# Dilated attention in a hybrid decoder layer: distant keys by residue modulo four

## The chip, the cores and the metric

The kernel runs on one core of a Trainium2 chip. The metric is the device time of one execution in microseconds; a program's time is the median of several runs. Five engines work side by side and wait for each other by semaphores: TensorE (PE in the profile, with PEld for the loading of weights), VectorE (DVE), ScalarE (ACT), GpSimd (POOL) and SyncE (SP), whose queue issues most DMA transfers.

## What is computed

One decoder layer over a sequence of 1024 positions with 1024 channels. A projection of the normalised input feeds three groups of heads: four HGRN2 heads, four heads of dilated attention and four RWKV-7 heads. Their outputs go through an output projection, then a gated MLP with a short convolution, a gate with a per-layer embedding, and a final norm. The part that matters here:

```python
SW_PATTERNS = ((128, 1), (512, 4), (2048, 16))

def dilated_window_mix(q_raw, k_raw, v_raw):
    ...
    for window, dil in SW_PATTERNS:
        o, lse = banded_causal_attention(stride_gather(q, dil), stride_gather(k, dil),
                                         stride_gather(v, dil), window // dil)
        outs.append(stride_scatter(o, B_, dil))
        lses.append(stride_scatter(lse, B_, dil))
    wts = jax.nn.softmax(jnp.stack(lses, 0), axis=0)
    o = jnp.sum(wts[..., None] * jnp.stack(outs, 0), axis=0)
```

A query at position l meets, in the first pattern, all keys from l-128 to l; in the second, every fourth key back to l-512; in the third, every sixteenth back to l-2048, which is beyond the start of the sequence. The mixture by softmax denominators equals one softmax over all keys, in which a key counts as often as there are patterns that hold it (0 to 3). So further back than 128 positions a query meets only keys whose distance is a multiple of four.

## The kernel before

All work in this kernel is laid out by channel: tiles are 128 channels (two attention heads of 64) by positions. The input projection's products (`dp`, `zp`) are split into three products of a reduced fp32 type; the attention works on plain fp32.

**Where attention stands.** `phase_mix` (line 310) first runs RWKV, then interleaves four generators by hand (line 331): A and B are two chains of HGRN2 heads, C is the attention (`swa`, line 1238), F the last four columns of the input projection (`project_late`, line 526), which fill TensorE in the first half. `TURNS` (line 347) says in which of 38 rounds C gets a turn, `LATE` (line 348) in which F does. This interleaving is the program order; a scheduler then orders each engine's instructions from it and may move ready ones ahead. Behind the interleaving stands the output projection, whose first row (`first_rows`, line 336, tile `dp`) takes the heads in the order of `OUT` (line 334).

**Attention.** The heads come in two pairs, p = 0 and 1. For each pair eight query blocks of 128 positions (`qb` 0 to 7) are run through three steps, one turn apart:

- `swa_scores` (line 1285): query block `qb` against all keys from 0 to the end of its own block, for two heads (`HEADS`: partitions 0 to 63 and 64 to 127), into two PSUM tiles `swq` of the large kind (`dps`, two buffers in all). On DVE one instruction (line 1303) adds a mask, `swmask`, and finds the row's minimum; on ACT one (line 1305) takes the exponential and its sum, giving `lg`. The mask is -1e30 for keys that no pattern holds, and 8 log(count) for the others. All of `swmask` is a window into one array of 1024 columns, moved by 128 per block.
- `swa_turn` (line 1310): `lg` is transposed by TensorE in pieces of 128x128 (tile `swt`, the small PSUM kind `mx`, four buffers) and copied to `pT`, the first 512 keys by ACT and the rest by DVE.
- `swa_values` (line 1323): values (`sV`, turned once per pair in `swa_values_in`, line 1273) times `pT`, one matmul per key block and head, into `swo`, then copied by DVE to the output tile `ob`. After every fourth block `swa_out` (line 1338) divides by the sums, which `widen` and `spread2` (lines 185 and 190, tile `swd`) bring to every channel.

Per head pair this makes 36 pairs of 128x128 blocks, of which a large part holds mostly keys that are masked out.

**Queries and keys.** Queries, keys and values come from the input projection: `project_done` (line 485) scales a projected column by the norm's factor into `zst`, stores it to memory, and `swa_load` (line 1269) brings it back. Columns 24 and 27 are the queries of the two pairs.

Of the kernel before, what the change touches and what calls it, by code (L numbers as in the profile page):

```python
# [10 lines left out]
F32 = mybir.dt.float32  # L11
# [3 lines left out]
ALU = mybir.AluOpType  # L15
# [27 lines left out]
def shape_constants():  # L43
# [14 lines left out]
    c[:, CC_RU:CC_RU + P] = same & (ff % 64 >= 32) & (pp % 64 < 32)  # L58
    u = np.arange(T)[None, :]
    d = pp - (u - 896)  # L60
    cnt = ((d >= 0) & (d <= 128)).astype(np.float64)
# [18 lines left out]
class Trunk:  # L80
# [229 lines left out]
    def phase_mix(self):  # L310
# [8 lines left out]
        with self.pool("hg") as slots, self.pool("sw") as sp:  # L319
            self.slots, self.NSLOT = slots, 11  # L320
            with tc.issue_after(self.squared):
                self.hgrn_setup()
            self.sp = sp
            self.swmask = sp.tile([P, T], F32, name="swmask")
# [155 lines left out]
    def pending(self, what):  # L480
        go = self.pend.pop(what, None)
        if go:
            go()

    def project_done(self, j, ps, staged=False):
        t = self.keep.tile([P, T], F32, tag="zst", name=self.nm("zst"), bufs=2)
        kind = (j - 8) % 4 if j < 24 else 2
        parts = [(t, ps, self.R)]
        if j < 24 and kind < 3:
# [36 lines left out]
    def project_late(self, js):  # L526
# [3 lines left out]
        for i, j in enumerate(js):  # L530
# [6 lines left out]
            for hf in (0, 1):  # L537
# [3 lines left out]
                r = self.R[:, hf * HT:(hf + 1) * HT]  # L541
                self.finish(kind, t[:, dst], *((ps[:, ::-1], r[:, ::-1]) if turn and hf else (ps, r)))
                nc.sync.dma_start(d[:, dst], t[:, dst])
# [694 lines left out]
    def swa(self, sp):  # L1238
# [6 lines left out]
        for p in (0, 1):  # L1245
            d = ds[p]
            for qb in range(10):
# [5 lines left out]
                if qb == p:  # L1253
                    self.swa_values_in(d)
                if qb > 1:
                    fin = self.swa_values(sp, d, *pend.pop(0))
                if 0 < qb < 9:
                    pend[-1:] = [self.swa_turn(sp, *pend[-1])]
                if qb < 8:
# [13 lines left out]
    def swa_values_in(self, d):  # L1273
        nc, vc = self.nc, d["v"]
        V = self.sp.tile([P, T], F32, tag="sd", name=self.nm("sV"), bufs=1)
        for hf in (0, 1):
# [3 lines left out]
            nc.scalar.copy(V[:, hf * HT:(hf + 1) * HT], pt)  # L1280
        d["V"] = V.rearrange("p (b c) -> p b c", c=P)

    HEADS = slice(0, 64), slice(64, 128)

    def swa_scores(self, sp, d, qb):
        nc = self.nc
        qi, nk = qb % 4, (qb + 1) * P
        if qi == 0:
            d["den"] = sp.tile([P, 16], F32, tag="sden", name=self.nm("sden"), bufs=2)
        den = d["den"]  # L1290

        pq = [self.dps.tile([P, T], F32, tag="dp", name=self.nm("swq")) for _ in self.HEADS]
        for b in range(0, nk, HT):
            w = min(HT, nk - b)
            for h, hs in enumerate(self.HEADS):
                nc.tensor.matmul(pq[h][:, b:b + w], d["q"][hs, qb * P:nk], d["k"][hs, b:b + w], start=True, stop=True)  # L1296
        lgs = []
        for h in (0, 1):
            lg = sp.tile([P, T], F32, tag="lg", name=self.nm("lg"), bufs=4)
            nm = den[:, 8 + 2 * qi + h:9 + 2 * qi + h]  # L1300

            m0 = 896 - qb * P
            nc.vector.tensor_tensor_reduce(lg[:, :nk], pq[h][:, :nk], self.swmask[:, m0:m0 + nk],
                                           -0.125, 3e38, ALU.add, ALU.min, nm)
# [4 lines left out]

    def swa_turn(self, sp, qb, den, lgs):  # L1310
        nc, nk, pT = self.nc, (qb + 1) * P, []
        for lg in lgs:
            t = sp.tile([P, T], F32, tag="pT", name=self.nm("pT"), bufs=2)
            pT.append(t)
            for b in range(0, nk, HT):
                w = min(HT, nk - b)
                pt = self.mxp.tile([P, HT], F32, tag="mx", name=self.nm("swt"))
                for kb in range(w // P):
                    nc.tensor.transpose(pt[:, kb * P:(kb + 1) * P], lg[:, b + kb * P:b + (kb + 1) * P], self.ident)  # L1319
                (nc.vector.tensor_copy if b else nc.scalar.copy)(t[:, b:b + w], pt[:, :w])  # L1320
        return qb, den, pT

    def swa_values(self, sp, d, qb, den, pT):
        nc = self.nc
        if qb == 0:
            d["o"] = self.keep.tile([P, T], F32, tag="zst", name=self.nm("ob"), bufs=2)
        o = d["o"]
        po = self.mxp.tile([P, P], F32, tag="mx", name=self.nm("swo"))

        for kb in range(qb + 1):  # L1330
            for h, hs in enumerate(self.HEADS):
                nc.tensor.matmul(po[hs, :], d["V"][:, kb, hs], pT[h][:, kb * P:(kb + 1) * P], start=kb == 0, stop=kb == qb)  # L1332
        nc.vector.tensor_copy(o[:, qb * P:(qb + 1) * P], po)
        if qb % 4 == 3:
# [3 lines left out]
    def swa_out(self, d, qb, o, den):  # L1338
# [3 lines left out]
        os = slice((qb - 3) * P, (qb + 1) * P)  # L1342
        nc.vector.tensor_tensor(o[:, os], o[:, os], pd, ALU.mult)
        if qb == 7:
# [704 lines left out]
```

## Time and profile before

| | us |
|---|---|
| median of 3 runs | 1426.47 |
| lowest and highest run | 1426.33, 1426.6 |
| the profiled execution | 1426.57 |
| its span (first to last instruction) | 1424.8 |

The mean granted clock of TensorE in the profiled execution is 0.997. The profile comes from that one execution. A line names the source line, the engine, the operation, the tile written and the tiles read, the shape and the count; the busy time of a group is the union of its instructions. "idle before" is what the engine waited for just ahead of them. Two records of a matmul stand for one matmul of plain fp32 operands, one record for a transpose or a matmul of the reduced type. `64*128` ahead of a shape is the part of the array in use: rows (contracted partitions) by columns (output partitions).

### The profile page before, as it was taken

Reading aid. Unit: us, or ns where it says so; the run is one execution under the profiler, and the core shown is the slowest. Engines: PE = TensorE matmul, PEld = TensorE weight load, DVE = VectorE, ACT = ScalarE, POOL = GpSimd, SP = SyncE. Lnnn points to the kernel's source line nnn. Section 1 sums busy time; section 2 is a strip of 40 time slices with the busy share of each in tenths; the row PEclk is TensorE's granted clock in tenths of the full one; section 3 lists DMA queues with packets and bytes.
Section 4 is the critical chain, followed back from the end, with each engine's and each line's share of the span. In section 5 each row is a group of like instructions: output and inputs, shape, how many; then the busy total and the mean of one; then the engine's idle time right before and its main releaser. Section 6 shows DMA issues by size and latency. Waiting matters only on the chain.

```text
span 1424.8 us, 20276 instructions
## 1 busy us (share of the span) xinstructions
PE 1410.4 (99%) x7406; PEld 1166.4 (82%) x7406; DVE 1089.2 (76%) x1679; ACT 648.5 (46%) x1207; POOL 446.1 (31%) x360
## 2 busy tenths in 40 slices
PE   9999999999999999999999999999999999999997
PEld 7888887888877877888888888888888888888886
DVE  7667576674786787448998889888988799777685
ACT  7531443214535676335544444343444445455552
POOL 2221442124421331222245445454543000002343
PEclk9999999999999999999999999999999999999998
DMA  5233021230350320374332333333233973352343
GB/s 212 78 97 104 31 75 59 85 115 30 105 185 31 119 82 31 123 262 156 140 113 83 100 105 102 112 111 103 97 108 115 347 257 102 105 164 59 121 151 135
DMA packets 80019, 167.84 MB, mean 118 GB/s; under 512 B 20080, under 2 KB 22256, under 8 KB 79920
## 3 DMA queue, kind: packets, MB, share of 16 engines
q1 hardware_dynamic: 66144, 145.97, 31.0%
q10 hardware_dynamic: 12832, 17.04, 3.6%
q0 software_dynamic: 944, 3.54, 0.7%
q8 instruction: 58, 0.95, 0.3%
q14 instruction: 41, 0.34, 0.1%
HBM read 120.12 MB, written 46.40 MB: 117 GB/s over the span
## 4 chain that ended last, share of the span: by engine, by line
PE 93%; DVE 3%; ACT 2%; DMA 1%; issue 1%; POOL 0%; SPq 0%; DVEq 0%; ACTq 0%; POOLq 0%
PE bg L1465 17%; PE bv L1465 13%; PE dp L130 9%; PE dp L132 8%; PE dp L134 8%; PE bg L1787 7%; PE bv L1787 7%; PE hsc L1124 2%; PE swq L1296 2%; PE bv L130 1%; PE bv L132 1%; PE bv L134 1%; PE swt L1319 1%; PE swo L1332 1%; PE bg L132 1%; PE bg L130 1%
## 5 line engine op out<-in xcount | busy, mean ns | idle before, releaser
L130 PE MATMUL dp<-xh,whi 128*128 128x512 f32 x544 | 196.8, 407 | 0.0
L132 PE MATMUL dp<-xl,whi 128*128 128x512 f32 x544 | 188.0, 391 | 1.0 <-DVE xl L393 1.0
L134 PE MATMUL dp<-xh,wlo 128*128 128x512 f32 x544 | 188.3, 391 | 0.0
L108 POOL TENSOR_TENSOR wlo<-wraw,whi 128x512 fp32r<-128x512 f32 x63 | 89.3, 1421 | 245.2 <-ACT whi L106 237.4
L108 POOL TENSOR_TENSOR wlo<-raw,whi 128x512 fp32r<-128x512 f32 x84 | 135.7, 1634 | 73.9 <-ACT whi L106 73.9
L1465 PE MATMUL bg<-t,whi 128*128 128x512 f32 x352 | 132.4, 389 | 0.0
L106 ACT CAST whi<-wraw 128x512 fp32r<-128x512 f32 x120 | 72.6, 617 | 119.2 <-PE dp L132 73.8
L134 PEld LDWEIGHTS dp<-xh,wlo 128*128 128x128 f32 x544 | 102.1, 188 | 22.1 <-issue 0.5
L132 PEld LDWEIGHTS dp<-xl,whi 128*128 128x128 f32 x544 | 102.1, 188 | 20.8 <-DVE xl L393 1.6
L130 PEld LDWEIGHTS dp<-xh,whi 128*128 128x128 f32 x544 | 101.5, 188 | 21.5 <-issue 3.0
L108 POOL TENSOR_TENSOR wlo<-s,whi 128x512 fp32r<-128x512 f32 x44 | 66.0, 1500 | 161.6 <-ACT whi L106 150.7
L106 ACT CAST whi<-s 128x512 fp32r<-128x512 f32 x66 | 39.0, 621 | 123.2 <-PE bg L1465 115.2
L1787 PE MATMUL bg<-t,whi 128*128 128x512 f32 x308 | 94.9, 389 | 0.0
L1787 PE MATMUL bv<-t,whi 128*128 128x512 f32 x308 | 94.9, 389 | 0.0
L106 ACT CAST whi<-raw 128x512 fp32r<-128x512 f32 x88 | 52.6, 619 | 91.6 <-issue 48.5
L175 POOL TENSOR_TENSOR rst<-rst,mhalf 128x4 f32<-128x4 f32 (+1 forms) x9 | 10.3, 1145 | 219.7 <-DVE rst L173 219.7
L1465 PEld LDWEIGHTS bg<-t,whi 128*128 128x128 f32 x352 | 66.1, 188 | 13.7
L1783 ACT CAST t<-t 128x512 fp32r<-128x512 f32 x77 | 47.8, 622 | 47.7 <-PE bv L1787 29.4
L108 DVE TENSOR_TENSOR wlo<-wraw,whi 128x512 fp32r<-128x512 f32 x57 | 43.6, 768 | 31.5 <-ACT whi L106 27.6
L1787 PEld LDWEIGHTS bv<-t,whi 128*128 128x128 f32 x308 | 57.8, 188 | 12.0
L1787 PEld LDWEIGHTS bg<-t,whi 128*128 128x128 f32 x308 | 57.8, 188 | 11.9
L1465 PE MATMUL bg<-t,wlo 128*128 128x512 f32 x176 | 67.2, 389 | 0.0
(448 smaller groups left out, 3609.2 us busy)
## 6 DMA issues: line engine op xcount, KB each, us to landing
raw<-in_ffn_up_dram SPq DMA_DIRECT2D x44, 512.0 KB, 3.6
wraw<-in_w_in_dram SPq DMA_DIRECT2D x29, 512.0 KB, 3.6
z<-zst SPq DMA_DIRECT2D x18, 512.0 KB, 2.7
gb<-ct SPq DMA_DIRECT2D x33, 256.0 KB, 2.3
t<-gb SPq DMA_DIRECT2D x33, 256.0 KB, 2.8
t<-gt SPq DMA_DIRECT2D x33, 256.0 KB, 2.7
zl<-z SPq DMA_DIRECT2D x16, 512.0 KB, 4.7
wraw<-in_ple_gate_dram SPq DMA_DIRECT2D x16, 512.0 KB, 3.5
```

Source lines behind the costliest of these rows:

```text
L106: nc.scalar.copy(hi, src)
L108: eng.tensor_tensor(lo, src, hi.bitcast(F32), ALU.subtract)
L130: nc.tensor.matmul(ps[hf], wh, xh[hf], start=first, stop=False)
L132: nc.tensor.matmul(ps[hf], wh, xl[hf], start=False, stop=False)
L134: nc.tensor.matmul(ps[hf], wl, xh[hf], start=False, stop=last)
L1124: nc.tensor.matmul(sc[:, c, :], ks[:, c * P:(c + 1) * P], view(qt, c * P, [2 * n, 64 // n], [HT + n, 2], [1, n]), start=True, stop=True)
L1296: nc.tensor.matmul(pq[h][:, b:b + w], d["q"][hs, qb * P:nk], d["k"][hs, b:b + w], start=True, stop=True)
L1319: nc.tensor.transpose(pt[:, kb * P:(kb + 1) * P], lg[:, b + kb * P:b + (kb + 1) * P], self.ident)
L1332: nc.tensor.matmul(po[hs, :], d["V"][:, kb, hs], pT[h][:, kb * P:(kb + 1) * P], start=kb == 0, stop=kb == qb)
L1465: nc.tensor.matmul(ps, w[part == 2][:, s], X[k][part == 1], start=start and k == part == 0, stop=k == 3 and part == 2, skip_group_check=no ...
L1783: nc.scalar.copy(xh, x)
L1787: nc.tensor.matmul(ps[m], wt[part == 2][:, m * P:(m + 1) * P], (xh, xl)[part == 1], start=k == part == 0, stop=k == NK - 1 and part == 2)
```

## The change

Only the attention changes, with the layout of its queries.

**Far keys.** For a query block `qb` of 2 or more, keys two or more blocks back are met by residue modulo four: the 32 queries of a block whose position has residue r meet only the keys of residue r, a quarter of them. `qb // 2 * 64` keys per residue are taken, so 64, 64, 128, 128, 192, 192 for `qb` 2 to 7. Per block that is four residues by two heads, eight matmuls of 64 rows by 32 columns; keys are read with a step of four. For even `qb` this takes in the block before the query's own, which the mask then leaves out.

**Near keys.** The block's own keys and the block before are met densely, 256 keys (128 for `qb` 0). Far and near logits stand side by side in one PSUM tile, 128 to 448 columns per head, the two heads in one tile of the large kind. One masked minimum and one exponential run over both.

**Queries in classes.** Within each block of 128, queries are stored by residue (`classes`), so that a residue's 32 queries are neighbours. The scaling of columns 24 and 27 writes them so, and the result's copy and division (`plain`) put the positions back.

**Turning and values.** Transposes fall from 144 to 92. `swa_values_in` also turns the values by residue, into `F` (16 transposes and four copies over both pairs). Values are taken for two blocks at a time: the key block that both meet goes as one matmul of 256 columns, the two others as 128 each, the far ones as 64 columns (32 queries of two blocks) per residue and head. The first head's turned weights are copied by ACT, the second's by DVE.

The core of the diff (line numbers in the rows below it are those of the changed kernel):

```diff
     def swa_scores(self, sp, d, qb):
         nc = self.nc
-        qi, nk = qb % 4, (qb + 1) * P
+        qi, w = qb % 4, 64 * (qb // 2)
+        near = slice(max(qb - 1, 0) * P, (qb + 1) * P)
+        nk = w + near.stop - near.start
...
-        pq = [self.dps.tile([P, T], F32, tag="dp", name=self.nm("swq")) for _ in self.HEADS]
-        for b in range(0, nk, HT):
-            w = min(HT, nk - b)
+        pq = self.dps.tile([P, 2, HT], F32, tag="dp", name=self.nm("swq"))
+        self.uid += 1
+        for r in range(4 if w else 0):
             for h, hs in enumerate(self.HEADS):
-                nc.tensor.matmul(pq[h][:, b:b + w], d["q"][hs, qb * P:nk], d["k"][hs, b:b + w], start=True, stop=True)
+                q0 = qb * P + 32 * r
+                nc.tensor.matmul(pq[32 * r:32 * r + 32, h, :w], d["q"][hs, q0:q0 + 32], d["k"][hs, r:4 * w:4],
+                                 start=True, stop=True)
+        for h, hs in enumerate(self.HEADS):
+            nc.tensor.matmul(pq[:, h, w:nk], d["q"][hs, qb * P:(qb + 1) * P], d["k"][hs, near], start=True, stop=True)
...
+        cols = [w + b * P for b in range(2 if qb else 1)] + [b * P for b in range((w + 64) // P)]
+        for lg, t, copy in zip(lgs, d["pT"], (nc.scalar.copy, nc.vector.tensor_copy)):
+            pt = self.mxp.tile([P, HT], F32, tag="mx", name=self.nm("swt"))
+            for i, c in enumerate(cols):
+                nc.tensor.transpose(pt[:, i * P:(i + 1) * P], lg[:, c:c + P], self.ident)
+            copy(t[:, qb % 2, :len(cols) * P], pt[:, :len(cols) * P])
...
+            nc.tensor.matmul(po[hs], d["V"][:, q0, hs], both, start=True, stop=False)
+        for e, kb in ((0, q0 - 1), (1, q0 + 1))[not q0:]:
             for h, hs in enumerate(self.HEADS):
-                nc.tensor.matmul(po[hs, :], d["V"][:, kb, hs], pT[h][:, kb * P:(kb + 1) * P], start=kb == 0, stop=kb == qb)
-        nc.vector.tensor_copy(o[:, qb * P:(qb + 1) * P], po)
+                nc.tensor.matmul(po[hs, e, :], d["V"][:, kb, hs], pT[h][:, e, e * P:(e + 1) * P], start=False,
+                                 stop=not w and e == 1)
+        for f in range((w + 64) // P):
+            n = min(P, w - f * P)
+            for r in range(4):
+                c = (2 + f) * P + 32 * r
+                for h, hs in enumerate(self.HEADS):
+                    nc.tensor.matmul(po[hs, :, 32 * r:32 * r + 32], d["F"][:n, f, r, hs], pT[h][:n, :, c:c + 32],
+                                     start=False, stop=(f + 1) * P >= w and r == 3)
+        os = slice(q0 * P, (q0 + 2) * P)
+        nc.vector.tensor_copy(self.plain(o[:, os]), self.classes(po.rearrange("p e q -> p (e q)")))
```

The scheduler also orders the rows anew. The first place is on PE, in the second head pair, at the scores of query block 6. Before, two tiles (`swq_5065` and `swq_5066`) hold the two heads; `hsc` are scores of an HGRN2 head, `swd` the spreading of the sums:

```order
L1296 MATMUL swq_5065<-zl_4085,zl_4348 128x512
L1124 MATMUL hsc_5037<-qt_4609,ks_4972 128x128 x4
L1124 MATMUL hsc_5048<-qt_4963,ks_4991 128x128 x4
L1296 MATMUL swq_5066<-zl_4085,zl_4348 128x512
L193 MATMUL swd_5059<-cst,par 128x128 x4
L1296 MATMUL swq_5065<-zl_4085,zl_4348 128x384
L1296 MATMUL swq_5066<-zl_4085,zl_4348 128x384
```

In the changed kernel, the same engine around block 6 (`swq_5049`) and the end of block 5 (`swq_4974`); `32x128` and `32x192` are far matmuls of one residue and head, `128x256` near ones:

```order
L1324 MATMUL swq_4974<-zl_4100,zl_4341 32x128
L1351 MATMUL swt_4924<-cst,lg_4848 128x128 x3
L1324 MATMUL swq_4974<-zl_4100,zl_4341 32x128
L1138 MATMUL hsc_4929<-qt_4577,ks_4877 128x128 x4
L1324 MATMUL swq_4974<-zl_4100,zl_4341 32x128 x6
L1327 MATMUL swq_4974<-zl_4100,zl_4341 128x256 x2
L1324 MATMUL swq_5049<-zl_4100,zl_4341 32x192 x8
L1327 MATMUL swq_5049<-zl_4100,zl_4341 128x256 x2
```

Block 6 stands together now, eight far matmuls and two near ones, where the heads' first 512 keys were parted before; block 5's eight far matmuls are in three pieces with other work between them. In the whole new order, six of the twelve far sets are cut, into nine pieces more than sets, and four of the sixteen near pairs are parted.

The second place is on PE too, where the first row of the output projection (`dp`) begins, in the second head pair. Before, around the turning of block 6 (`swt_5205` to `swt_5223`) and the outputs of an HGRN2 head (`hpo`):

```order
L1319 MATMUL swt_5205<-cst,lg_5071 128x128 x4
L1319 MATMUL swt_5211<-cst,lg_5071 128x128 x3
L130 MATMUL dp_5503<-xh_4701,whi_5499 128x512
L130 MATMUL dp_5503<-xh_4685,whi_5499 128x512
L1319 MATMUL swt_5217<-cst,lg_5074 128x128 x4
L1319 MATMUL swt_5223<-cst,lg_5074 128x128 x3
```

In the changed kernel, around the turning of the same block (`swt_5178` and `swt_5184`):

```order
L137 MATMUL dp_5441<-xl_4670,whi_5437 128x512
L137 MATMUL dp_5441<-xl_4654,whi_5437 128x512
L1351 MATMUL swt_5178<-cst,lg_5060 128x128 x4
L139 MATMUL dp_5441<-xh_4669,wlo_5439 128x512
L1351 MATMUL swt_5184<-cst,lg_5063 128x128 x4
L1215 MATMUL hpo_5193<-hV_5078,hS_4607 128x128
L139 MATMUL dp_5441<-xh_4653,wlo_5439 128x512
L135 MATMUL dp_5441<-xh_4671,whi_5437 128x512
L135 MATMUL dp_5441<-xh_4655,whi_5437 128x512
L137 MATMUL dp_5441<-xl_4672,whi_5437 128x512
```

More of the output projection stands ahead of the last steps of the mixing: 40 of its matmuls come before the last transposes `vt` of the HGRN2 heads, where 24 did. The order of the SP queue is the same as before, and GpSimd's differs in the place of three instructions.

More of the change, by code (lines that the diff above doesn't have):

```diff
@@ L58, in shape_constants, with far @@
     c[:, CC_RU:CC_RU + P] = same & (ff % 64 >= 32) & (pp % 64 < 32)
-    u = np.arange(T)[None, :]
-    d = pp - (u - 896)
+    qi, qr = pp % 32, pp // 32
+    near = P + 4 * qi + qr - np.arange(2 * P)[None, :]
+    def far(ds):
+        return np.concatenate([P * d + 4 * (qi - np.arange(32)[None, :]) for d in ds], axis=1)
+    d = np.concatenate([far((6, 5, 4, 3, 2)), np.full((P, 32), -1), near, far((7, 6, 5, 4, 3, 2)), near], axis=1)
     cnt = ((d >= 0) & (d <= 128)).astype(np.float64)
@@ L323, in phase_mix @@
             self.sp = sp
-            self.swmask = sp.tile([P, T], F32, name="swmask")
+            self.swmask = sp.tile([P, 2 * self.SWM], F32, name="swmask")
             nc.scalar.dma_start(self.swmask, self.a["swm"])
@@ L487, in project_done @@
         kind = (j - 8) % 4 if j < 24 else 2
-        parts = [(t, ps, self.R)]
+        parts = [(self.classes(t), self.plain(ps), self.plain(self.R)) if j in (24, 27) else (t, ps, self.R)]
         if j < 24 and kind < 3:
@@ L541, in project_late @@
                 r = self.R[:, hf * HT:(hf + 1) * HT]
-                self.finish(kind, t[:, dst], *((ps[:, ::-1], r[:, ::-1]) if turn and hf else (ps, r)))
+                if j in (24, 27):
+                    self.finish(kind, self.classes(t[:, dst]), self.plain(ps), self.plain(r))
+                else:
+                    self.finish(kind, t[:, dst], *((ps[:, ::-1], r[:, ::-1]) if turn and hf else (ps, r)))
                 nc.sync.dma_start(d[:, dst], t[:, dst])
@@ L1308, in swa_scores @@
         return den, lgs
[L1310 to L1321, printed above, removed]
@@ L1323, in swa_values, with swa_turn @@
-    def swa_values(self, sp, d, qb, den, pT):
+    def swa_turn(self, sp, d, qb, den, lgs):
+        nc, w = self.nc, 64 * (qb // 2)
+        if qb % 2 == 0:
+            d["pT"] = [sp.tile([P, 2, HT], F32, tag="pT", name=self.nm("pT"), bufs=3) for _ in lgs]
+        else:
+            self.uid += 2
+        cols = [w + b * P for b in range(2 if qb else 1)] + [b * P for b in range((w + 64) // P)]
[4 more added lines that the diff above has]
+            copy(t[:, qb % 2, :len(cols) * P], pt[:, :len(cols) * P])
+        return qb, den, d["pT"]
@@ L1324, in swa_values @@
+    def swa_values(self, sp, d, q0, den, pT):
         nc = self.nc
-        if qb == 0:
+        if q0 == 0:
             d["o"] = self.keep.tile([P, T], F32, tag="zst", name=self.nm("ob"), bufs=2)
+            self.uid += 1
         o = d["o"]
-        po = self.mxp.tile([P, P], F32, tag="mx", name=self.nm("swo"))
-        for kb in range(qb + 1):
-            for h, hs in enumerate(self.HEADS):
-                nc.tensor.matmul(po[hs, :], d["V"][:, kb, hs], pT[h][:, kb * P:(kb + 1) * P], start=kb == 0, stop=kb == qb)
@@ L1334, in swa_values @@
+        qb = q0 + 1
         if qb % 4 == 3:
```

36 lines of the change are left out of this document (29 added, 7 removed).

## Prediction

> **What bounds the kernel now.** I read the page first, then the stretch in which attention runs, then the order of single groups there.
>
> ```profile
> span 1424.8 us, 20276 instructions
> PE 1410.4 (99%) x7406; PEld 1166.4 (82%) x7406; DVE 1089.2 (76%) x1679; ACT 648.5 (46%) x1207; POOL 446.1 (31%) x360
> PE 93%; DVE 3%; ACT 2%; DMA 1%; issue 1%; POOL 0%; SPq 0%; DVEq 0%; ACTq 0%; POOLq 0%
> ```
>
> TensorE (PE) is busy for 99% of the span and carries 93% of the chain that ended last, so a microsecond of PE work that disappears shortens the kernel unless something else holds PE up in its place. The attention runs from 403 to 575 us. The view by windows gives, for each stretch, its length and then the busy time of PE, PEld, DVE, ACT and POOL:
>
> ```profile
> 403.00:500.00 97.00, 96.73 (x671) 78.60 (x671) 73.73 (x148) 57.09 (x122) 24.72 (x22) 1.00 0.28 101
> 500.00:575.00 75.00, 72.82 (x577) 57.04 (x574) 60.67 (x136) 51.27 (x136) 21.48 (x19) 1.00 0.18 61
> 520.00:540.00 20.00, 19.85 (x137) 13.76 (x136) 18.34 (x38) 13.51 (x30) 5.37 (x5) 1.00 0.09 27
> ```
>
> The first stretch is the first pair of heads, with projections as filling; PE has no gap and VectorE (DVE) has 23 us to spare. The second is the second pair, without projections; DVE is busy for 60.7 of 75 us, and for 18.3 of 20 in its densest part. That is the engine to fear once PE work is gone. The groups of attention on PE, by shape (busy us, mean ns of one; each matmul of two fp32 operands leaves two records):
>
> ```profile
> L1296 PE MATMUL swq<-zl,zl 64*128 64x512 f32 x48 | 18.9, 639 | 0.0
> L1296 PE MATMUL swq<-zl,zl 64*128 64x384 f32 x16 | 4.5, 522 | 0.0
> L1296 PE MATMUL swq<-zl,zl 64*128 64x256 f32 x16 | 2.7, 415 | 0.0
> L1296 PE MATMUL swq<-zl,zl 64*128 64x128 f32 x16 | 1.9, 310 | 0.0
> L1319 PE MATMUL swt<-cst,lg 128*128 128x128 f32 x144 | 20.4, 281 | 1.0 <-ACT pT L1320 0.8
> L1332 PE MATMUL swo<-pT,sV 128*64 128x128 f32 x288 | 19.3, 278 | 0.0
> ```
>
> Scores take 28.0 us, the turning of the weights 20.4, the values 19.3. A row's busy time runs into the next group's, because matmuls are pipelined, so I price by the time from one group's start to the next one's, in the timeline (start, length):
>
> ```profile
> 523.01 1.12 PE L1296 MATMUL swq<-zl,zl 64*128 64x512 f32 x2
> 524.06 0.66 PE L1222 MATMUL vt<-cst,ho 128*128 128x128 f32 x4
> 524.65 0.49 PE L1296 MATMUL swq<-zl,zl 64*128 64x128 f32 x4
> 525.07 0.88 PE L1332 MATMUL swo<-pT,sV 128*64 128x128 f32 x12
> 525.88 1.09 PE L1319 MATMUL swt<-cst,lg 128*128 128x128 f32 x8
> ...
> 527.79 1.13 PE L1296 MATMUL swq<-zl,zl 64*128 64x512 f32 x4
> 528.85 1.16 PE L1124 MATMUL hsc<-qt,ks 128*128 128x128 f32 x8
> ...
> 531.92 0.70 PE L1296 MATMUL swq<-zl,zl 64*128 64x256 f32 x4
> 532.56 1.09 PE L1332 MATMUL swo<-pT,sV 128*64 128x128 f32 x16
> ...
> 544.97 1.04 PE L1149 MATMUL vt<-cst,zl 128*128 128x128 f32 x8
> 545.85 1.04 PE L1155 MATMUL vt<-cst,hk 128*128 128x128 f32 x8
> ...
> 552.14 1.53 PE L1332 MATMUL swo<-pT,sV 128*64 128x128 f32 x24
> 553.60 0.98 PE L1319 MATMUL swt<-cst,lg 128*128 128x128 f32 x7
> ```
>
> Five things are read here. Two heads' scores of 512 keys (x4 at 527.79) take 1.06 us to the next start, and one head's alone (x2 at 523.01) takes 1.05: heads that stand together in the order share the array, and a head that the order has parted from its twin costs a whole pair. A pair of 256 keys takes 0.64, of 128 keys 0.42, so 64 keys more cost 0.11 and going in and out of this shape about 0.2. A transpose takes 0.88/8 = 0.11. Values: 12 records take 0.81, 24 take 1.46, so one costs 0.054, half of a whole-array pass of the same 128 columns, and a group 0.15 beside: the two column halves of the array also work side by side. The score rows overlap the next by 0.07 (1.12 against 1.05) in the 26 runs that the order has of them, so scores really take 28.0 - 1.8 = 26.2 us; values, in 16 groups, 19.3 - 1.1 = 18.2.
>
> **The change part by part.** *Near scores.* Per head pair there are eight query blocks; one meets 128 keys, seven meet 256. Over both pairs: 14 x 0.64 + 2 x 0.42 = 9.8. In the new order four of these pairs stand apart and pay a second 0.64: 2.6. Together 12.4.
>
> *Far scores.* Six query blocks per head pair, each with eight matmuls (four residues by two heads) of 64 rows, 32 columns and 64, 128 or 192 keys (two blocks each). The trace has no 32-column tile. If all eight work abreast, a set costs what a pair of that width does: 0.31, 0.42, 0.53, so 4 x 1.26 = 5.0; the order cuts six sets into nine extra pieces, at 0.42 each 3.8: 8.8. If only the two heads share the array and the residues follow one another, a set costs 0.2 + 4 x 0.11, 0.22 or 0.33: 13.0, and with the cuts' entries (9 x 0.2) 14.8. If all eight follow one another, 0.2 + 8 x the same: 23.5 + 1.8 = 25.3. I take 8.8, because the two nearest rows (row halves in swq, column halves in swo) both show tiles abreast. Scores then go from 26.2 to 21.2: -5.0.
>
> [...]
>
> *Turning.* 144 transposes become 92: -52 x 0.11 = -5.7. The values of the far keys, regathered by residue, add 16: +1.8. Their source is read with a step of four; were that to cost double, 1.8 more.
>
> *Values.* 288 records become 216. 56 are as before (3.0), 32 are twice as wide (32 x 0.108 = 3.5), 128 have 64 columns. For these the trace has rows of the same tile and width:
>
> ```profile
> 382.20 0.69 PE L1000 MATMUL pn<-XV,W 128*64 128x64 f32 x16
> 382.72 0.64 PE L1006 MATMUL pyo<-XV,W 128*64 128x64 f32 x16
> ```
>
> 0.52/16 = 0.033 each, so 4.2. Eight groups instead of 16 at 0.15 make 1.2; four sets use only 64 rows of the array, another shape, at 0.2: 0.8. Sum 12.7 against 18.2: -5.5.
>
> PE's sum: -5.0 - 5.7 + 1.8 - 5.5 = -14.4 us.
>
> *The other engines.* They matter only where they take over. The masked minimum on DVE goes from widths 128 to 1024 to widths 128 to 448:
>
> ```profile
> L1303 DVE CUSTOM_DVE_ANT_0 lg<-swq,swmask 128x1024 f32<-128x1024 f32 x4 | 4.9, 1224 | 1.4 <-PE swq L1296 1.4
> ...
> L1303 DVE CUSTOM_DVE_ANT_0 lg<-swq,swmask 128x512 f32<-128x512 f32 x4 | 2.6, 678 | 0.0
> L1303 DVE CUSTOM_DVE_ANT_0 lg<-swq,swmask 128x384 f32<-128x384 f32 x4 | 2.1, 545 | 0.0
> ```
>
> On the line through these rows (545 ns at 384, 1224 at 1024: 1.06 ns per column) the eight widths go from 6.0 us per head of a pair to 4.0, over four heads -8 us. Exponentials and copies on ACT shrink likewise; ACT is not near its limit. DVE pays back something, because queries now stand in classes of four and three kinds of operation read or write with a step of 32 elements. The nearest row is a copy with such a step:
>
> ```profile
> L763 DVE COPY Ub<-Tb 64x1024 f32<-64x1024 f32 x2 | 3.6, 1778 | 0.1
> L495 DVE TENSOR_TENSOR zst<-dp,rstd 128x1024 f32<-128x1024 f32 x4 | 4.9, 1224 | 8.8 <-PE dp L134 8.8
> ```
>
> At 1.74 ns an element instead of 1.2, the two scalings of the queries lose 0.55 us each, the four of the outputs (512 wide) 0.3 each, and the eight copies of the values' results (256 wide, for sixteen of 128) about nothing net: at most +2.3. The scalings of the queries lie before 403 us, beside projections that keep PE busy, so they cost nothing; without that cover 1.1. DVE is 5 to 6 us lighter over the attention, 3 in each stretch.
>
> *New waits.* In the second stretch PE gets some 7 us lighter (half of 14.4) and DVE only 3, so PE will wait more. Its present waits there show the kind:
>
> ```profile
> 555.90 0.98 PE L1319 MATMUL swt<-cst,lg 128*128 128x128 f32 x7 [0.84 <-ACT pT L1320]
> ...
> 565.41 1.16 PE L1124 MATMUL hsc<-qt,ks 128*128 128x128 f32 x8 [0.71 <-ACT pT L1320]
> ```
>
> Against that, the scores of a block now hold one PSUM buffer of the large kind instead of both, and the new order moves some 16 more matmuls of the output projection ahead into this stretch, where they fill gaps. The bounds are 0 (filled) and 4 us (DVE's relief alone counts there). I charge 2.5, three waits like the two shown. The regrouped values make DVE's copy wait for two blocks; behind it on DVE stand the heads' mask and product steps, which the same 2.5 covers.
>
> Forecast: -14.4 + 2.5 = -11.9. The profiled execution took 1426.57 us (1424.8 of span and 1.8 around it), 0.1 above the median of the runs; so 1414.7.
>
> **Rivals.** *B, the quarter tiles do not work abreast.* Then the far scores cost 14.8 instead of 8.8, PE's sum is -8.4, and with 2 us of waits the time is 1420. Against it: one swo record costs 0.054 although both halves use the same rows. [...]
>
> *C, DVE takes over in the second stretch.* There DVE's 60.7 us become 57.7 and its gaps of 14 us stay, since they come from the recurrent heads' steps between DVE, ACT and PE; the stretch then shrinks by 3 instead of 7.2. With the first stretch's 7.2 that is -10.2, and 1 us for the regrouped values' waits at the end: 1417.5. For it speaks 18.3 of 20 us; against it, the filling by output projection.
>
> *D, slower.* Every matmul of a 32-column tile waits for the array to empty, as a change of shape does now (0.2). Its place is line 1324 of the new kernel: 96 x 0.2 + 4 x 8 x (0.11 + 0.22 + 0.33) = 19.2 + 21.1 = 40.3 us instead of 8.8, so -11.9 + 31.5: 1446. It decides the sign from 8.8 + 11.9 = 20.7 us, 0.22 us per far matmul. Against it: both kinds of half tiles go without such a wait.
>
> *E, no change.* The eight tiles follow one another without that wait (25.3): -14.4 + 16.5 = +2.1, and PE then has no new waits: 1428.7. Both heads' sharing in swq speaks against it.
>
> **How the numbers follow.** A measurement of this kernel can tell about 0.2%, 2.9 us. The forecast gets 0.60 with its own range of 1411 to 1419 (waits from 0 to 4, cuts and steps priced one way or the other), B 0.15, C 0.12, D 0.08, E 0.05. The forecast, B and C are faster: 0.87; E is the same, 0.05; D is slower, 0.08. The range reaches from 1409 (all tiles abreast, no waits, and three of the present waits gone) to 1422 (B with 3.5 us of waits); it leaves out D and E.
>
> **What would show it.** Right: far records of one set that start a few ns apart, and a set that takes 0.3 to 0.6 us; 92 + 16 transposes; values at about 13 us; PE waits in the second stretch under 5 us; the end of attention some 12 us earlier, and everything behind it unchanged in length. B shows as sets of 0.6 to 1.5 us in four steps, D as 0.2 between records. C shows as PE waiting for DVE after 500 us. A scaling or copy with a step above 1.8 ns an element would make DVE's term wrong; PE waits over 7 us in the first stretch would make the whole argument wrong.

## The result and the profile after

The changed kernel takes 1417.03 us (median of 6 runs, 1415.26 to 1417.50) against 1426.43 (6 runs, 1426.33 to 1426.60): ratio 0.9932, 95% interval 0.9920 to 0.9945, or 9.4 us less. The forecast was 1414.7, with a range of 1409 to 1422 and 0.87 for faster. The profiled execution took 1417.01 us. Its page, in the rows that answer to those of before:

```profile
span 1415.3 us, 20337 instructions
PE 1399.3 (99%) x7458; PEld 1157.8 (82%) x7458; DVE 1085.8 (77%) x1671; ACT 634.9 (45%) x1193; POOL 446.7 (32%) x360
PE 93%; DVE 3%; ACT 1%; DMA 1%; issue 1%; POOL 1%; SPq 0%; DVEq 0%; ACTq 0%; POOLq 0%
```

PE still carries the chain and is 11.1 us less busy, of 9.5 us of span. The windows of attention, and behind them four microseconds of the first stretch (length, then busy PE, PEld, DVE, ACT, POOL, the granted clock, DMA):

```profile
403.00:500.00 97.00, 94.67 (x722) 76.94 (x721) 73.52 (x150) 52.33 (x121) 26.73 (x23) 0.98 0.30 105
500.00:575.00 75.00, 74.43 (x645) 59.08 (x643) 59.33 (x135) 45.05 (x133) 22.20 (x19) 1.00 0.17 57
418.00:422.00 4.00, 3.76 (x18) 3.16 (x19) 3.44 (x10) 2.87 (x10) 0.20 (x1) 0.57 0.11 41
```

Before, PE had 0.3 us of gaps in the first stretch and 2.2 in the second. Now it is the other way round: 2.3 us of gaps in the first, 0.6 in the second. And the clock of PE is 0.57 for a while in the first. The groups of attention on PE, by shape:

```profile
L1351 PE MATMUL swt<-cst,lg 128*128 128x128 f32 x92 | 14.6, 288 | 1.8 <-ACT lg L1336 1.8
L1327 PE MATMUL swq<-zl,zl 64*128 64x256 f32 x56 | 12.6, 428 | 0.0
L1324 PE MATMUL swq<-zl,zl 64*32 64x192 f32 x64 | 6.1, 509 | 0.0
L1368 PE MATMUL swo<-pT,sV 128*64 128x256 f32 x32 | 5.2, 405 | 0.0
L1324 PE MATMUL swq<-zl,zl 64*32 64x128 f32 x64 | 4.5, 397 | 0.0
L1371 PE MATMUL swo<-pT,sV 128*64 128x128 f32 x56 | 4.4, 273 | 0.0
L1324 PE MATMUL swq<-zl,zl 64*32 64x64 f32 x64 | 2.9, 286 | 0.0
L1378 PE MATMUL swo<-pT,sF 64*64 64x64 f32 x64 | 2.7, 224 | 0.0
L1378 PE MATMUL swo<-pT,sF 128*64 128x64 f32 x64 | 2.5, 222 | 0.0
L1327 PE MATMUL swq<-zl,zl 64*128 64x128 f32 x8 | 1.0, 323 | 0.0
```

Line 1324 is the far scores, 1327 the near ones. The five rows of scores hold 27.1 us of busy time in 41 runs of the order; less 0.07 of overlap for each, 24.2. Near is 13.6 - 20 x 0.07 = 12.2, as priced (12.4); far is 13.5 - 21 x 0.07 = 12.0, where 8.8 had been priced. A far row of 192 keys has a mean of 509 ns, although a near one of 256 keys has 428: the far matmuls are slow for their width. Single sets in the timeline show the same:

```profile
428.02 0.43 PE L1324 MATMUL swq<-zl,zl 64*32 64x64 f32 x12
428.38 0.70 PE L1327 MATMUL swq<-zl,zl 64*128 64x256 f32 x4
...
431.51 0.67 PE L1324 MATMUL swq<-zl,zl 64*32 64x128 f32 x16
432.10 0.70 PE L1327 MATMUL swq<-zl,zl 64*128 64x256 f32 x4
```

A whole set of eight matmuls (16 records) of 128 keys takes 0.594 us to the near scores behind it. Its eight first records start at +0, 6, 13, 20, 26, 33, 40 and 46 ns: all eight tiles are under way at once. A set of 64 keys takes 0.371, of 192 keys 0.818, so 64 keys more cost 0.224, where the near scores had shown 0.11.

By the starts of marked groups, the first stretch (first scores of the first pair to first scores of the second) went from 95.8 to 92.6 us, -3.2. The second (to the last spreading of the denominators) went from 73.2 to 70.3, -3.0, and from there the output projection ends 3.6 earlier, because 16 more of its matmuls (0.227 each) stand inside the attention. So the second pair brought 6.6 us and the first, with 3.2, less than half of that. The first pair's loss is seen in one place. All engines, around 416 us:

```profile
413.07 0.70 PE L1327 MATMUL swq<-zl,zl 64*128 64x256 f32 x4
...
413.22 1.50 POOL L1140 TENSOR_TENSOR hk<-hk,zl 128x512 f32<-128x512 f32 x1 [1.99 <-PE hsc L1112]
413.45 2.02 DVE L1094 TENSOR_SCALAR hk<-zl 128x512 f32<-128x512 f32 x1
...
415.76 0.70 PE L1327 MATMUL swq<-zl,zl 64*128 64x256 f32 x4
416.00 1.20 DVE L1096 TENSOR_TENSOR qt<-zl,zl 128x1024 f32<-128x1024 f32 x1
417.13 0.41 DVE L1334 CUSTOM_DVE_ANT_0 lg<-swq,swmask 128x256 f32<-128x256 f32 x1
...
417.58 0.51 ACT L1336 ACTIVATE lg<-lg,sden 128x256 f32<-128x256 f32 x1 [2.00 <-DVE sden L1334]
...
418.24 0.65 PE L1351 MATMUL swt<-cst,lg 128*128 128x128 f32 x2 [1.78 <-ACT lg L1336]
...
418.82 0.42 PE L1324 MATMUL swq<-zl,zl 64*32 64x64 f32 x4
...
419.66 1.92 PE L1138 MATMUL hsc<-qt,ks 128*128 128x128 f32 x8
```

PE waits 1.78 us at 416.5 for the exponential of query block 1. That exponential waits for the masked minimum on DVE (line 1334), which starts at 417.13 although its scores (the near ones at 413.07; those at 415.76 belong to block 2) were done by 414. Ahead of it in the new DVE order stand the key copies (1094) and the query product (1096) of the second HGRN2 head, one copy of which took 2.02 us instead of its usual 0.41. In the kernel before, the same minimum stood ahead of both:

```profile
412.24 1.37 DVE L1100 COPY_PREDICATED hS<-cmask,hsc 128x512 f32<-128x512 uint8 x2
413.49 0.41 DVE L1303 CUSTOM_DVE_ANT_0 lg<-swq,swmask 128x256 f32<-128x256 f32 x1
```

Behind the wait PE runs at the lower clock: the eight hsc records take 1.92 us where they usually take about 1.1. The four records of far scores at 418.82 are a piece that this order cut from block 3's set.

### The profile page after: what moved, and what is told of

It reads as the page before. It is cut to its first block, busy times and chain, and to the rows that moved or that the text cites. A ratio compares the mean times of both kernels' runs of the same rounds, so it can differ in the third digit from the quotient of the medians.

```text
span 1415.3 us, 20337 instructions
## 1 busy us (share of the span) xinstructions
PE 1399.3 (99%) x7458; PEld 1157.8 (82%) x7458; DVE 1085.8 (77%) x1671; ACT 634.9 (45%) x1193; POOL 446.7 (32%) x360
## 4 chain that ended last, share of the span: by engine, by line
PE 93%; DVE 3%; ACT 1%; DMA 1%; issue 1%; POOL 1%; SPq 0%; DVEq 0%; ACTq 0%; POOLq 0%
PE bg L1514 17%; PE bv L1514 13%; PE dp L135 9%; PE dp L137 9%; PE dp L139 9%; PE bg L1836 7%; PE bv L1836 7%; PE hsc L1138 2%; PE bv L135 1%; PE bv L139 1%; PE bv L137 1%; PE bg L139 1%; PE bg L135 1%; PE bg L137 1%; PE swt L1351 1%; PE swq L1324 1%
## 5 line engine op out<-in xcount | busy, mean ns | idle before, releaser
L1514 PEld LDWEIGHTS bg<-t,whi 128*128 128x128 f32 x352 | 66.2, 188 | 13.5
L1836 PEld LDWEIGHTS bv<-t,whi 128*128 128x128 f32 x308 | 57.9, 188 | 11.9
```

What stands on the lines that cost most here:

```text
L1514: nc.tensor.matmul(ps, w[part == 2][:, s], X[k][part == 1], start=start and k == part == 0, stop=k == 3 and part == 2, skip_group_check=no ...
L1836: nc.tensor.matmul(ps[m], wt[part == 2][:, m * P:(m + 1) * P], (xh, xl)[part == 1], start=k == part == 0, stop=k == NK - 1 and part == 2)
```

## Experiments

Two things had to be explained: the 3.4 us by which the first stretch fell short of the second pair, and the far scores' 3.2 us above their price. The theory for the first, called W here, is the place of that one minimum on DVE: a wait of about 1.8 us and as much again from the clock behind it.

**The minimum ahead of the second head's steps.** The DVE steps of the second head are issued only behind block 1's minimum:

```diff
+        with self.tc.issue_after(self.low_ins) if h == 1 else ExitStack():
             for a, b in ((0, HT), (HT, 0)):
                 nc.vector.tensor_scalar(k[:, a:a + HT], f[:, b:b + HT], -1.0, 1.0, ALU.mult, ALU.add)
             nc.vector.tensor_tensor(qt, q, f, ALU.mult)
...
+            if d["p"] == 0 and qb == 1:
+                self.low_ins = low.ins
```

> The key copies and the products of the second HGRN2 head are kept behind the masked minimum of query block 1 on VectorE. Theory W (the gain that is missing against the forecast is one wait of TensorE at 416 to 418 us for block 1's exponential, 1.9 us, and the half clock of 3.4 us behind it, 1.7 us): both go, 1417.0 becomes about 1413.5, and the granted clock rises to 0.997. Rival M (TensorE's work was mis-sized, and the wait only stands where another would): 1416 to 1417.

Measured: 1413.44 us (4 runs, 1413.36 to 1413.85), ratio 0.9909 (0.9894 to 0.9924), 3.6 less than the changed kernel. The same places in its windows and timeline:

```profile
403.00:500.00 97.00, 96.32 (x750) 78.76 (x749) 74.36 (x157) 55.20 (x129) 28.16 (x25) 1.00 0.32 110
500.00:575.00 75.00, 74.28 (x631) 58.25 (x629) 58.63 (x137) 42.87 (x133) 22.33 (x20) 1.00 0.15 50
```

```profile
414.44 0.42 DVE L1335 CUSTOM_DVE_ANT_0 lg<-swq,swmask 128x256 f32<-128x256 f32 x1
...
416.57 0.66 PE L1354 MATMUL swt<-cst,lg 128*128 128x128 f32 x4
417.06 1.12 PE L1139 MATMUL hsc<-qt,ks 128*128 128x128 f32 x8
```

The minimum runs 2.7 us earlier, PE goes on without a gap, the clock stays at 1.00. The first stretch is 89.1 us: -6.75 against the kernel before, as much as the second pair brings. W holds: with the minimum back in its place the 3.6 us are gone. A small part is not W's own, because block 3's far set, cut in the changed kernel (0.354 us for the piece and 0.357 for the rest), stands whole in this order (0.369).

**Idle matmuls in the wait.** To part the wait from the clock, eight matmuls of the identity matrix by itself fill the gap ahead of block 1's transposes; up to there DVE's order stays as it was.

```diff
+            if d["p"] == 0 and qb == 1 and lg is lgs[0]:
+                for _ in range(8):
+                    nc.tensor.matmul(pt[:, :P], self.ident, self.ident, start=True, stop=True)
```

> Eight matmuls without use stand on TensorE ahead of block 1's first transposes, so that the array has some work in the wait. The wait itself is left as it is. Theory W: the wait's end does not move, but the clock stays at full, so 1.0 to 1.7 us less: 1415.3 to 1416, clock 0.997. Rival (the half clock is not caused by the wait, or costs nothing because the stretch behind it waits anyway): 1417 to 1418.8, as the added 1.8 us are then simply longer.

Measured: 1415.49 us (4 runs, 1415.43 to 1415.55), 1.5 less than the changed kernel.

```profile
416.59 2.05 PE L1352 MATMUL swt<-cst 128*128 128x128 f32 x16
418.48 0.90 PE L1354 MATMUL swt<-cst,lg 128*128 128x128 f32 x4
419.22 1.13 PE L1138 MATMUL hsc<-qt,ks 128*128 128x128 f32 x8
```

The turning comes as late as before (418.48, against 418.24), but what follows runs at the full clock (1.00 from 418 to 422 us). This order, too, leaves block 3's far set whole, which saves 0.34 us; so about 1.2 of the 1.5 us are the clock. Of the 3.6 us the wait itself is then 1.8, the clock about 1.2 and the cut set 0.34; the last 0.3 lie in the order around them.

**Every far score twice.** This asks again, without the prices of the forecast, whether the eight tiles are abreast.

```diff
-        for r in range(4 if w else 0):
+        for r in (*range(4), *range(4)) if w else ():
```

> Every far score matmul is issued twice; the second pass writes the same numbers again. If all eight tiles of 32 columns work abreast, a set grows by 0.11, 0.21 or 0.32 us, 2.6 us in all, and cuts by the scheduler add up to 2: 1419.5 to 1422. If only the two heads share the array, 10.6 us more: 1427 or above.

Measured: 1424.58 us (10 runs, 1423.25 to 1424.99), 7.55 more: between the two expectations. The sets themselves decide:

```profile
431.99 1.12 PE L1324 MATMUL swq<-zl,zl 64*32 64x128 f32 x32
433.04 0.70 PE L1327 MATMUL swq<-zl,zl 64*128 64x256 f32 x4
```

A doubled set takes 1.05 us instead of 0.594. The second eight add 0.456, no more than 128 keys at 0.224 per 64, so all eight share the time. In the first pair, where the sets stay nearly whole, doubling cost 2.4 us. In the second the order cut the sets into 20 pieces instead of 13, and each piece costs nearly a whole set: 5.9 us. My expectation had not reckoned with the order.

**Both buffers for the scores, as before.** The prediction held that scores of a block in one PSUM buffer instead of two let more of the output projection in.

```diff
-        pq = self.dps.tile([P, 2, HT], F32, tag="dp", name=self.nm("swq"))
+        pq = [self.dps.tile([P, T], F32, tag="dp", name=self.nm("swq")) for _ in self.HEADS]
```

> The two heads' logits stand in two large PSUM buffers again, as before the change, so that one block's scores hold both. If the one free buffer is what lets the output projection fill TensorE in the second head pair (16 matmuls, 3.6 us), 2 to 4 us are lost: 1419 to 1421. If the waits there are few anyway and the fill only moves work, within 1 us of 1417.

Measured: 1414.14 us (4 runs, 1413.97 to 1414.38): not slower but 2.9 faster than the changed kernel. This edit also moved block 1's minimum on DVE ahead of the second head's query product, so that the wait of W is gone. It has to be compared with 1413.44, and then two buffers cost 0.7 us. Nine matmuls of the output projection fewer stand inside the attention (94.5 us instead of 92.4 from there to the start of its last one), but the second stretch is as much shorter (68.0 instead of 70.3), although PE waits once for 1.3 us in it; the 0.7 us come from the first (89.8 instead of 89.1), where PE waits for 0.6 and 0.3 us. So the fill that the single buffer lets in gained nothing by itself.

**Far keys read in one stretch.** The second question. The order of every engine is that of the kernel with the minimum ahead; only the addresses of the far keys differ.

```diff
-                nc.tensor.matmul(pq[32 * r:32 * r + 32, h, :w], d["q"][hs, q0:q0 + 32], d["k"][hs, r:4 * w:4],
+                nc.tensor.matmul(pq[32 * r:32 * r + 32, h, :w], d["q"][hs, q0:q0 + 32], d["k"][hs, r * w:r * w + w],
```

> Built on the kernel with the low minimum ahead (1413.44). The far scores read their keys in one stretch of w columns instead of one column in four; the attention is then over wrong far keys, and the order of every engine is the same. In the changed kernel a whole set of eight far tiles takes 0.37, 0.594 and 0.818 us at 64, 128 and 192 keys where 0.31, 0.42 and 0.53 had been expected: 64 keys more cost 0.224 and not 0.11, and the far scores take 12.0 us and not 8.8. Theory S: the step of four halves the rate at which the keys are read. Then sets of about 0.26 to 0.31, 0.37 to 0.42 and 0.48 to 0.53 us, far scores at 8.5 to 9.5 us, and 1410 to 1411 us. Rival T: four column tiles over the same rows share the reading of the keys at half rate whatever their step. Then the sets stay as they are, and the time is 1413.2 to 1413.7.

Measured: 1409.70 us (4 runs, 1409.51 to 1410.05), ratio 0.9884 (0.9869 to 0.9898), 3.7 less than with the step.

```profile
428.38 0.45 PE L1325 MATMUL swq<-zl,zl 64*32 64x128 f32 x16
428.75 0.70 PE L1328 MATMUL swq<-zl,zl 64*128 64x256 f32 x4
```

The set of 128 keys takes 0.38 us instead of 0.594, those of 64 and 192 take 0.272 and 0.486: 64 keys more cost 0.107, the near scores' price. The step of four in the keys had halved the rate, and not the four column tiles.

**Far keys with a step of two.** In the same order:

```diff
-                nc.tensor.matmul(pq[32 * r:32 * r + 32, h, :w], d["q"][hs, q0:q0 + 32], d["k"][hs, r:4 * w:4],
+                nc.tensor.matmul(pq[32 * r:32 * r + 32, h, :w], d["q"][hs, q0:q0 + 32], d["k"][hs, r % 2:r % 2 + 2 * w:2],
```

> Built on the kernel with the low minimum ahead (1413.44). The far scores read every second key column instead of every fourth, so the attention is over wrong far keys; the order of every engine is the same. A step of four gave whole sets of 0.37, 0.594 and 0.818 us and 1413.44 us, no step 0.272, 0.38 and 0.486 us and 1409.70 us. [...] Rival M, any step halves the rate: 1413.2 to 1413.7. Rival N, the rate falls with the step: between, about 1411 to 1412. [...]

Measured: 1410.39 us (4 runs, 1410.05 to 1411.43), where the kernel before took 1427.07 on the same chip, 0.6 more than in the runs of the step of four: 16.7 less than before, against 16.5 without a step and 13.0 with a step of four. The far matmuls of the two kernels (duration of one: lowest, median, highest), the step of two first:

```profile
L1325 PE MATMUL swq<-zl,zl x192: 214/286/361, 416.0 to 533.2; 64*32 64x64 f32 x64, 64*32 64x128 f32 x64, 64*32 64x192 f32 x64
```

And the step of four, in the kernel with the minimum ahead:

```profile
L1325 PE MATMUL swq<-zl,zl x192: 276/398/532, 415.6 to 536.2; 64*32 64x64 f32 x64, 64*32 64x128 f32 x64, 64*32 64x192 f32 x64
```

A median of 286 ns against 398, and 281 without a step. By width, one far matmul takes 229, 285 and 341 ns in the mean at 64, 128 and 192 keys, without a step 228, 281 and 335, with the step of four 285, 397 and 509: 64 keys more cost a record 56, 54 and 112 ns. A step of two is almost free, a step of four halves the rate. The two steps exclude that any step costs and that the cost rises evenly; why four costs and two does not is not shown.

**The values one block at a time.** Each product over two query blocks becomes two:

```diff
-            nc.tensor.matmul(po[hs], d["V"][:, q0, hs], both, start=True, stop=False)
+            for e in (0, 1):
+                nc.tensor.matmul(po[hs, e, :], d["V"][:, q0, hs], both[:, e, :], start=e == 0, stop=False,
...
-                    nc.tensor.matmul(po[hs, :, 32 * r:32 * r + 32], d["F"][:n, f, r, hs], pT[h][:n, :, c:c + 32],
+                    for e in (0, 1):
+                        nc.tensor.matmul(po[hs, e, 32 * r:32 * r + 32], d["F"][:n, f, r, hs], pT[h][:n, e, c:c + 32],
```

> Built on the kernel with the low minimum ahead (1413.44). The values' products over two query blocks are split into one product per block: 32 matmuls of 256 columns become 64 of 128 and 128 of 64 columns become 256 of 32. The prediction priced a matmul by its columns (0.108 for 256, 0.054 for 128, 0.033 for 64). Theory by columns: a matmul of 32 columns takes half of one of 64, so the sum grows by little, 0 to 1 us: 1413.4 to 1414.5. Rival, a floor: a matmul of 32 columns takes as long as one of 64 because its weights set the pace; then 128 more at 0.033 are 4.2 us more: 1417 to 1418.

Measured: 1416.92 us (4 runs, 1416.71 to 1417.23), 3.5 more.

```profile
L1384 PE MATMUL swo<-pT,sF 64*64 64x32 f32 x128 | 4.6, 221 | 0.0
L1384 PE MATMUL swo<-pT,sF 128*64 128x32 f32 x128 | 4.5, 222 | 0.0
```

A matmul of 32 columns lasts 221 or 222 ns, as one of 64 does (224, 222), and the two rows grow from 5.2 to 9.1 us: 0.041 us of busy time a record at 64 columns, 0.036 at 32. The floor holds: from 64 to 32 columns next to nothing is won (why is not shown), and taking two blocks in one product is worth 3.5 us of the change.

**TensorE in the order of the program.** With and without the change, the scheduler's order of PE is replaced by that of the program text, in which all sets and pairs stay whole. First on the kernel with the minimum ahead:

```diff
-            interleave(order, {"A": A, "B": B, "C": self.swa(sp), "F": self.project_late(self.rest)})
+            with tc.manual_schedule(engines={mybir.EngineType.PE}):
+                interleave(order, {"A": A, "B": B, "C": self.swa(sp), "F": self.project_late(self.rest)})
```

> Built on the kernel with the low minimum ahead (1413.44), with TensorE's instructions kept in the order of the program: all far sets and all near pairs stay whole, and the output projection no longer fills gaps one matmul at a time. Theory P, the parted pieces are a pure cost: near 4 x 0.64 = 2.6 us less, far 7.1 instead of 12.0 us, together 7.5 less: 1405 to 1407. Rival F, the pieces stand where TensorE would wait else: then PE waits appear in the second stretch and take back as much or more: 1413 or above. Between the two, 1408 to 1412, both hold in part, and the PE waits in the stretch from 400 to 566 us say how much.

Measured: 1417.60 us (4 runs, 1416.30 to 1417.94), 4.2 more. The far scores fell from 12.0 to 7.2 us as worked out, but PE now waits in the attention (us in total, times, longest):

```profile
PE hsc L1140 <- DVE qt L1144: 3.2, 2, 2.3
PE hsc L1140 <- ACT hV L1166: 1.2, 1, 1.2
...
```

Twelve waits, 9.6 us together, where the kernel with the minimum ahead has three of 0.2 to 0.3. From 500 to 575 us its mean granted clock is 0.98, where the kernel with the minimum ahead has 1.00, so a part of the loss is the clock. In the scheduler's order the parted pieces stand where PE would wait otherwise. But the edit fixes all of PE's order in the mixing, so that it does not price the pieces alone. Then the same edit on the kernel before:

> The kernel before (1426.45) with TensorE's instructions kept in the order of the program. There 26 runs of scores hold the 16 pairs; whole, they would cost 12 x 1.06 / 2 x 2 = 12.7 (512 keys and above), 3.4, 2.6 and 1.7 us, 20.4 instead of 26.1. Theory P: 5 to 6 us less, 1420 to 1422, so that of the gain of the change a part only makes good what the order lost. Rival F: waits take its place, 1426 or above.

Measured: 1433.58 us (4 runs, 1433.08 to 1434.56), 7.3 more than before, with waits of the same kind, the longest of them 3.6 us, and again a mean clock of 0.98 from 500 to 575 us (1.00 before). Between these two, in which no scheduler places PE's work in the mixing, the change and the earlier minimum together are worth 16.0 us.

**Keys sorted by residue, for good.** The step is taken out of the far scores by a copy that sorts 768 keys of each pair by residue; to make room the weights have three buffers instead of four.

```diff
+            self.nc.scalar.copy(d["kr"], d[n][:, :768].rearrange("p (j r) -> p r j", r=4))
...
-                nc.tensor.matmul(pq[32 * r:32 * r + 32, h, :w], d["q"][hs, q0:q0 + 32], d["k"][hs, r:4 * w:4],
+                nc.tensor.matmul(pq[32 * r:32 * r + 32, h, :w], d["q"][hs, q0:q0 + 32], d["kr"][hs, r, :w],
```

> Built on the kernel with the low minimum ahead (1413.44). ScalarE copies 768 keys of each head pair, sorted by residue, into a tile of their own, from which the far scores read w columns in one stretch; to make room the weights have three buffers instead of four. Reading in one stretch alone gave 1409.70, 3.74 less. Theory: two copies of some 1 us on ScalarE (54 us of 97 busy) are hidden, the order parts the sets as before, and three buffers do; 1409.5 to 1410.5. Rival: the copy of the second pair or the missing buffer delays an exponential that TensorE waits for, and the time is 1411.5 to 1414.

> As the kernel with the keys sorted into a tile of their own, with the copy on GpSimd instead of ScalarE. If the copy is hidden either way: within 0.5 us of the other. If GpSimd's work beside VectorE stretches VectorE's operations (one took 2.02 us instead of 0.41 beside GpSimd in the changed kernel): 0.5 to 2 us slower than the other.

> The kernel with the low minimum ahead (1413.44), with three buffers for the weights instead of four and nothing else. If the fourth buffer is not needed: 1413.2 to 1413.8. If TensorE's turning waits for a buffer: 1 to 3 us more, with a PE wait for ACT's exponentials in the trace.

Measured: three buffers alone 1413.51 us (4 runs, 1413.03 to 1414.18), no different from 1413.44. The copy on ScalarE 1411.97 (5 runs, 1410.70 to 1416.84), on GpSimd 1409.34 (4 runs, 1408.96 to 1411.85), ratio 0.9884 (0.9870 to 0.9897). The copies on GpSimd:

```profile
L1292 POOL COPY kr<-zl x2: 1611/1619/1627, 396.2 to 455.7; 128x768 f32<-128x768 f32 x2
```

They are hidden: in the same runs this version takes 4.2 us less than the one with three buffers alone, where the run without a step had won 3.7, and 17.2 us less than the kernel before; it is 7.7 below the changed kernel. On ScalarE the second copy takes 1.57 us in front of work of the recurrent heads, and PE then waits 1.6 us for their hV. GpSimd was 2.6 us faster in the median, which neither expectation had allowed. DVE's work was hardly stretched in the stretch that holds the second copy: from 403 to 500 us it was busy for 75.03 us in 162 instructions, and for 74.36 in 157 with the minimum ahead.

## Why the prediction was right, and where it was not

The direction and the size came out, 9.4 us less against 11.9, inside the range. The mechanism was the forecast one, and two of its terms, the far scores and the new waits, had the wrong size. That the total still came within 2.5 us is luck in part: the waits were charged to another stretch and another cause, and the turning and the values made good some of what the far scores cost.

*Near scores, turning, values.* Near 12.2 against 12.4. By starts, and in the kernel with the minimum ahead, the turning of the weights fell by 7.1 us, from 19.5 to 12.4, where 5.7 had been forecast. Of these, 0.7 are waits within it or behind it that became shorter (1.1 before, 0.4 now). The other 6.4 make 0.12 a transpose, where a run of eight had shown 0.11; the groups are as many as before (19) and shorter. The values fell by 6.1 where 5.5 had been forecast. F's 16 transposes, read with the step of four, last 272 to 286 ns, where most others take 272 or 273, but for one of 387 behind a wait. There the stepped tile is the stationary operand, and the step cost next to nothing: the eight weight loads of 128 columns took 196 to 219 ns, where the values' loads without a step took 139 to 143, and their transposes, but for that one, are followed after 118 to 122 ns instead of 108 to 110.

*Far scores.* "All eight work abreast" was right: starts 6 to 7 ns apart, and doubling a set adds only its columns. "A set costs what a pair of that width does" failed: 0.37, 0.594 and 0.818 instead of 0.31, 0.42 and 0.53, 12.0 us instead of 8.8. The step of the prediction that failed is this price. The row for it came from near scores that read their keys one after the other; the far ones read every fourth. I weighed that step for F's transposes and forgot it for the keys, where it was the moving operand. The runs without a step and with a step of two show that it was the step: 64 keys more cost a far record 112 ns at a step of four, 56 at a step of two and 54 without one.

*New waits.* 2.5 us were charged, in the second stretch. There they were next to nothing: 0.6 us of gaps, less than before, with the output projection's matmuls between the attention's. They came in the first stretch, which the prediction had taken to be free since PE had no gap and DVE had 23 us to spare: 1.8 us of wait for one minimum that had lost its place on DVE, and about 1.2 for the clock behind it. "Behind it on DVE stand the heads' mask and product steps" looked at what would queue behind attention's work; what came about was attention's own step queued behind the heads'. The order of the changed kernel shows it; the prediction read that order on PE alone. Without that wait the time is -13.0 us against a PE sum of -14.4: far scores 3.2 worse, turning and values 2.0 better (0.7 of it shorter waits).

*DVE's steps.* The copies of the values' results read PSUM with their step at no cost, and the output scalings too:

```profile
L1381 DVE COPY ob<-swo 128x256 f32<-128x256 f32 x8 | 3.4, 420 | 2.0 <-PE swo L1378 2.0
L1392 DVE TENSOR_TENSOR ob<-ob,swd 128x512 f32<-128x512 f32 x4 | 2.7, 678 | 0.0
```

The same operations took 414 to 420 ns for 256 columns (the copies of the turned weights) and 676 for 512 (the output scalings before) without a step. The scalings of the queries, which write with it, are slower than priced:

```profile
L506 DVE TENSOR_TENSOR zst<-dp,rstd 128x1024 f32<-128x1024 f32 x4 | 6.5, 1627 | 8.8 <-PE dp L139 8.8
```

Two of the four are as before (1224), so the other two take 2030 ns: 0.8 us more each, above the 1.8 ns an element at which I had called the term wrong. They lie before 403 us beside the projections, as argued; the first scores start at 403.45 instead of 403.12, so at most 0.3 us of it shows.

*Signs.* Two of the signs that were named did not come. A set of 192 keys took 0.818 us, above the 0.3 to 0.6 that was to speak for the forecast and inside the 0.6 to 1.5 of B; only the starts and the doubled sets told the two apart. And the attention ended 5.9 us earlier, not some 12, and the stretch behind it became 3.6 us shorter, because more of the output projection stood inside the attention.

*Rivals.* B, D and E needed tiles that are not abreast; none came. The four residues of a head use the same 64 rows, and still all eight matmuls of the set at 431.51 us start within 47 ns. All sixteen weight loads of that set start within 75 ns, while its first matmul runs for 391. C needed DVE to become the bound behind 500 us; no wait of the attention there passes 0.3 us.

## What to carry to other kernels

When work is taken off the bounding engine, read the new order on the other engines too, at the places where the bounding one had no gap: one short step that falls behind two long ones can cost a quarter of the gain (3.6 of 13.0 us here). Price a matmul by a row with the same step in its moving operand, and if the step is four in fp32, try sorting the operand once on an engine whose copy delays nobody (here GpSimd, and not ScalarE). Pieces that an order cuts from a set may look like waste and be the filling of waits; undo them on trial only.

## What the runs showed of the hardware

Eight tiles of 64 rows by 32 columns started 6 to 7 ns apart and ran at once (391 ns each), also where four share their rows. A step of four fp32 elements in the moving operand halved the rate (0.224 against 0.107 us per 64 keys, two records a matmul), a step of two made the mean matmul at most 2% longer (229, 285 and 341 ns against 228, 281 and 335); in the stationary operand a step of four cost about 0.01 us a transpose (0.12 instead of 0.11 from start to start). A matmul of two fp32 operands with 64 columns of weights took as long at 32 columns (221 and 222 ns) as at 64 (224 and 222). A DVE multiplication that writes SBUF with a step of 32 fp32 elements took 2.03 us instead of 1.22, while reading PSUM with that step cost next to nothing (420 ns against 414 to 420, 678 against 676).

A wait of 1.8 us of PE was followed by 3.4 us at half the clock (0.50), worth about 1.2 us, and with eight idle matmuls in the wait the clock stayed at 1.00 from 418 to 422 us, where the changed kernel had 0.57. The mean clock was 0.996 in five of the changed kernel's six runs, and 0.997 in the sixth, which took 1415.26. With every far score twice, a wait of 1.6 us came ahead of a clock of 0.58 from 420 to 424 us. In the two kernels with TensorE in the order of the program, whose longest waits were 2.3 and 3.6 us, the clock was 0.98 over the 75 us from 500. In the run with the copy on ScalarE there was a wait of 1.6 us too, and its mean clock was 0.998, as high as in any run, so the length of the wait alone did not decide.

A DVE key copy took 2.02 us in the changed kernel, 1.82 with every far score twice and 1.34 with both buffers; the other seven of each kernel took 0.42 in the mean. In the changed kernel GpSimd had been running since 413.22 us, and ran on to 414.72, when the copy started at 413.45. That GpSimd is the cause was not tried.
